# MLP down passes: seven products in place of eight for the first two input blocks and each pair of output groups

## The chip, the cores and the metric

The kernel runs on one core of a Trainium2 chip. Five engines of the core work side by side: TensorE (PE in the profile, with PEld for the loading of its stationary operand), VectorE (DVE), ScalarE (ACT), GpSimd (POOL) and SyncE (SP), which here only issues DMAs. Matmuls write to PSUM, eight banks of 128 x 512 float32; all else lies in SBUF. The metric is the device time of one execution in microseconds (us).

## The reference, cut to what matters

Two decoder layers on 256 tokens of width 2048 in float32. Each has a mixer and then a gated MLP with a short causal convolution:

```python
def conv_ffn(h, w_up, conv_w, conv_b, w_down):      # h: (1, 256, 2048)
    z = h @ w_up                                    # 2048 x 11264
    zp = jnp.pad(z, ((0, 0), (2, 0), (0, 0)))
    z = sum(conv_w[j] * zp[:, j:j + 256] for j in range(3)) + conv_b
    a, b = jnp.split(z, 2, axis=-1)
    return (jax.nn.silu(a) * b) @ w_down            # 5632 x 2048

for l in range(2):
    x = x + mixer(l, rms_norm(x, mix_norm[l]))
    x = x + conv_ffn(rms_norm(x, ffn_norm[l]), ...)
```

The change is in the last product, `(...) @ w_down`.

## The kernel before, in words

Float32 accuracy is built from three fast products. Each operand is split in a rounded high part and the rest (h and l), and a product is ah*bh + ah*bl + al*bh, three matmuls. Activations are split once and kept; weights are split as they come: ScalarE makes `wh` (line 185) and VectorE makes `wl = w - wh` (line 186). `halves` does both, `weights` (196) loads a tile of 512 KB on SP's queue and calls it.

`three` (162) hands out the buffers w, wh and wl of one weight tile and counts a turn. In the MLP (`deep["more"] == 2`), from turn 13 on, turns that are 1 or 3 modulo 5 take them from the pool fw (2 buffers of each kind), the others from wp (5 buffers of w, 3 of wh and of wl).

`project_four` (356) computes 256 tokens x 512 output columns: two PSUM banks, one for each half T of the tokens, and steps of two input blocks of 128. A step loads one weight tile (2 input blocks x 512 columns) and issues 2 (T) x 2 (input blocks) x 3 = 12 matmuls of 128x512, in lines 369 to 371. The stationary operand is the activation block, the moving one the weights.

`ffn` (1298) is the MLP of a layer. `up(j0)` computes four hidden blocks with two calls of project_four (8 steps each) and lets convolution, gate and split run beside later work, as generators that `tick` moves on by one piece each step; the result is appended to `hid`, a list of split hidden blocks of 128 features. `down(k0, hid, ...)` (1406) takes n of them, and for each of the four groups q of 512 output columns runs project_four over the n blocks (n/2 steps) and adds the two banks to `y` in SBUF (the first pass copies them, line 1424, later ones add, line 1426). STEPS sets the order: 4 ups, a down pass of 12 blocks; 3 ups, 12 blocks; 4 ups, 12 blocks; and the last 8 blocks. In the last pass `add_y` transposes each finished group of y and adds it to the residual x; in the last pass of the second MLP, group 3 is computed another way, block by block with `project` (301), and its sum of the earlier passes is added by `add_y(3, False)` ahead of the pass.

The order on each engine is the compiler's, from the dependences that it finds. Besides them `in_order` chains all w loads, all wh and all wl in written order, and `held` keeps an operation behind the last wl written so far.

Of the kernel before, what the change touches and what calls it, by code (L numbers as in the profile page):

```python
# [55 lines left out]
def tile_trunk(ctx: ExitStack, tc: tile.TileContext, x, pp_d, cst_d, mlev_d, msk_d,  # L56
# [105 lines left out]
    def three(n):  # L162
# [7 lines left out]
        w = wpool.tile([P, n], F32, tag="w", name=nm("w"), bufs=nw)  # L170
# [184 lines left out]
    def project_four(w4, acts, n, k0=0, ks=None, ps=None, more=False):  # L355

        begun = ps is not None
        ps = ps or [pm.tile([P, 512], F32, tag="pm", name=nm("pm")) for _ in range(2)]
        ks = ks or range(0, n, 2)
        for k in ks:  # L360
            tick()
            lo = (k0 + k) * P
            wh, wl = weights(w4[:, :, lo:lo + 2 * P].rearrange("m p c -> p m c"), 1024, 4)
            for T in range(2):
                for i in range(2):
                    a = acts(k + i) if callable(acts) else acts[k + i]
                    ah, al = a[:, T * P:(T + 1) * P], a[:, S + T * P:S + (T + 1) * P]
                    h, l = (by_rows(t, i) for t in (wh, wl))
                    PE.matmul(to_rows(ps[T]), ah, h, start=not begun and k + i == ks[0], stop=False)  # L369
                    PE.matmul(to_rows(ps[T]), ah, l, start=False, stop=False)  # L370
                    deep["mm"] = deep["last"] = PE.matmul(to_rows(ps[T]), al, h, start=False,  # L371
                                                          stop=not more and k + i == ks[-1] + 1)
        return ps

# [72 lines left out]
    class Norm:  # L447
        def __init__(self, col, turn=False):
# [4 lines left out]
            self.acc = cp.tile([P, S], F32, tag="acc", name=nm("acc"), bufs=2)  # L453
# [844 lines left out]
    def ffn(l, norm, last):  # L1298
        es = ExitStack()
        hp = es.enter_context(tc.tile_pool(name="fp", bufs=1))  # L1300
        deep.update(pool=es.enter_context(tc.tile_pool(name="fw", bufs=1)), turn=0, more=2)
        A = norm.a
# [7 lines left out]
        def four(j0):  # L1310
            ps = project_four(w_up[l, j0:j0 + 4], A, KT)
# [26 lines left out]
        def up(j0):  # L1338
# [12 lines left out]
            zb, eb = four(HT + j0)  # L1351
# [54 lines left out]
        def down(k0, hid, first, final):  # L1406
            n = len(hid)
            for q in range(4):
                if last and final and q == 3:
                    parts = None  # L1410
                    for m in range(4 * q, KT):
                        end = m == KT - 1
                        ps = project(w_dn[l, m], hid, chunks=(n,), k0=k0, parts=parts)
# [6 lines left out]
                ps = project_four(w_dn[l, 4 * q:4 * q + 4], hid, n, k0)  # L1420
# [6 lines left out]
                if final:  # L1427
                    add_y(q, True)

        j0, k0, hid = 0, 0, []  # L1430
        for g, (now, ahead) in enumerate(STEPS):
            while 4 * j0 < k0 + 4 * (now + ahead):
                up(4 * j0)
                j0 += 1
            n, final = 4 * now, g == len(STEPS) - 1
            if last and final:
                add_y(3, False)
            while len(hid) < k0 + n:
                tick()
            down(k0, hid[k0:k0 + n], g == 0, final)  # L1440
            k0 += n
        if last:
# [89 lines left out]
```

## Time and profile before

| | |
|---|---|
| median of 3 runs | 2166.17 us (2165.52 to 2166.69) |
| profiled execution, span | 2164.7 us |
| TensorE busy | 2160.1 us, 10736 matmuls |
| VectorE busy | 1610.1 us |
| ScalarE busy | 1307.4 us |
| GpSimd busy | 473.8 us |
| HBM read | 435.24 MB, 202 GB/s over the span |
| matmuls on `hid` (down passes), each of lines 369 to 371 | 688 |

The profile is of one execution. A group's row gives line, engine, operation, output and inputs, shapes and count, then the busy time in us and the mean in ns of one, then the idle time of the engine ahead of them and what ended it. A row of the timeline gives start and duration in us, engine, line and operation, and in brackets the idle time just before with its releaser. A row of the windows gives the window, then the busy time and count for PE, PEld, DVE, ACT and POOL, the granted clock, the DMA share and GB/s.

### The profile page before, as it was taken

The page shows a single profiled execution, that of the slowest core. Times are in us where ns is not written, and L with a number is a line of the kernel's source. Part 1 is how long each engine was busy: PE and PEld are TensorE (multiplying, and loading weights), DVE is VectorE, ACT ScalarE, POOL GpSimd, SP SyncE. Part 2 cuts the span into 40 slices and gives each one's busy share as a digit, 9 for nine tenths or more (in the row PEclk, how much of TensorE's full clock was granted, in tenths as well). Part 3 has the DMA queues.
Part 4 walks back from the last instruction along what each step waited for, and adds up shares of the span by engine and source line. Part 5 has one row for each costly group of instructions (what it writes and reads, how often), then busy time and mean ns, then how long its engine had stood idle before and what let it go on. Part 6 is the DMA issues. An engine that isn't in the chain of part 4 may idle for free.

```text
span 2164.7 us, 32175 instructions
## 1 busy us (share of the span) xinstructions
PE 2160.1 (100%) x10736; PEld 1895.8 (88%) x10736; DVE 1610.1 (74%) x2313; ACT 1307.4 (60%) x1888; POOL 473.8 (22%) x865
## 2 busy tenths in 40 slices
PE   9999999999999999999999999999999999999999
PEld 8888888888888888888888888888888888888888
DVE  7888768877577657776987787877786577667766
ACT  6677766666456545654565556766666466456652
POOL 0362231212012002111233443221211012012103
PEclk9999999999999999999999999999999999999999
DMA  8755777778667767776777767787777677766766
GB/s 300 224 171 174 223 222 237 237 227 241 216 214 223 225 209 216 225 239 207 249 232 222 246 201 214 221 243 220 242 234 224 201 236 217 227 214 211 243 213 194
DMA packets 492327, 483.60 MB, mean 223 GB/s; under 512 B 115360, under 2 KB 460080, under 8 KB 492032
## 3 DMA queue, kind: packets, MB, share of 16 engines
q1 hardware_dynamic: 465888, 453.41, 66.8%
q0 software_dynamic: 24832, 25.98, 5.2%
q10 hardware_dynamic: 1440, 2.15, 0.3%
q8 instruction: 84, 1.38, 0.3%
q14 instruction: 83, 0.68, 0.1%
HBM read 435.24 MB, written 2.11 MB: 202 GB/s over the span
## 4 chain that ended last, share of the span: by engine, by line
PE 100%; DMA 0%; ACT 0%; DVE 0%; SPq 0%; issue 0%; ACTq 0%
PE pm L369 27%; PE pm L370 27%; PE pm L371 27%; PE pm L350 5%; PE pm L352 4%; PE pm L351 4%; PE pm L236 1%; PE pm L315 1%; PE pm L318 1%; PE pm L260 1%; PE pm L325 0%; PE px L1110 0%; PE px L1163 0%; PE lv L829 0%; PE px L1107 0%; PE px L617 0%
## 5 line engine op out<-in xcount | busy, mean ns | idle before, releaser
L186 DVE TENSOR_TENSOR wl<-w,wh 128x1024 fp32r<-128x1024 f32 (+1 forms) x820 | 992.5, 1218 | 456.8 <-ACT wh L185 441.3
L185 ACT ACTIVATE wh<-w 128x1024 fp32r<-128x1024 f32 (+1 forms) x820 | 857.4, 1050 | 622.3 <-PE pm L371 449.3
L369 PE MATMUL pm<-wh,a 128*128 128x512 f32 x1728 | 655.7, 379 | 0.0
L370 PE MATMUL pm<-wl,a 128*128 128x512 f32 x1728 | 655.1, 379 | 0.0
L371 PE MATMUL pm<-wh,a 128*128 128x512 f32 x1728 | 654.9, 379 | 0.0
L391 POOL DMA_DIRECT2D zt<-tmp x413 | 223.6, 549 | 1135.2 <-DVE tmp L382 1047.6
L370 PEld LDWEIGHTS pm<-wl,a 128*128 128x128 f32 x1728 | 326.6, 189 | 46.7 <-DVE wl L186 0.7
L369 PEld LDWEIGHTS pm<-wh,a 128*128 128x128 f32 x1728 | 326.6, 189 | 46.3
L371 PEld LDWEIGHTS pm<-wh,a 128*128 128x128 f32 x1728 | 326.6, 189 | 46.3
L369 PE MATMUL pm<-wh,hid 128*128 128x512 f32 x688 | 260.8, 379 | 0.0
L370 PE MATMUL pm<-wl,hid 128*128 128x512 f32 x688 | 260.8, 379 | 0.0
L371 PE MATMUL pm<-wh,hid 128*128 128x512 f32 x688 | 260.8, 379 | 0.0
L350 PE MATMUL pm<-wh,a 128*128 128x512 f32 x416 | 158.5, 381 | 0.0
L351 PE MATMUL pm<-wl,a 128*128 128x512 f32 x416 | 157.7, 379 | 0.0
L352 PE MATMUL pm<-wh,a 128*128 128x512 f32 x416 | 157.7, 379 | 0.0
L370 PEld LDWEIGHTS pm<-wl,hid 128*128 128x128 f32 x688 | 130.0, 189 | 18.5
L369 PEld LDWEIGHTS pm<-wh,hid 128*128 128x128 f32 x688 | 130.0, 189 | 18.4
L371 PEld LDWEIGHTS pm<-wh,hid 128*128 128x128 f32 x688 | 130.0, 189 | 18.4
L1333 ACT ACTIVATE conv<-zt,pp 128x256 f32<-128x256 f32 x176 | 95.8, 589 | 64.1 <-DMA zt<-tmp 48.5
L391 POOL DMA_DIRECT2D turn<-tmp x159 | 86.4, 551 | 206.0 <-DVE tmp L382 173.0
L1334 DVE SCALAR_TENSOR_TENSOR conv<-zt,pp,conv 128x255 f32<-128x255 f32 x176 | 80.1, 480 | 47.8 <-ACT conv L1333 47.5
L382 DVE STREAM_TRANSPOSE tmp<-z 128x512 f32<-128x512 f32 x120 | 98.6, 855 | 6.1 <-ACT z L1319 4.2
(259 smaller groups left out, 2207.2 us busy)
## 6 DMA issues: line engine op xcount, KB each, us to landing
w<-in_w_up SPq DMA_DIRECT2D x352, 512.0 KB, 5.1
w<-in_w_dn SPq DMA_DIRECT2D x176, 512.0 KB, 4.9
w<-in_w_cqkv SPq DMA_DIRECT2D x96, 512.0 KB, 5.0
w<-in_w_abo SPq DMA_DIRECT2D x32, 512.0 KB, 4.9
w<-in_w_cg SPq DMA_DIRECT2D x32, 512.0 KB, 5.0
w<-in_w_co SPq DMA_DIRECT2D x32, 512.0 KB, 4.9
zt<-tmp SPq DMA_DIRECT2D x416, 32.0 KB, 2.5
zt<-tmp POOLq DMA_DIRECT2D x413, 32.0 KB, 2.5
```

The lines of the kernel that those rows point to most:

```text
L185: r = deep["wh"] = SC.activation(wh, w, AF.Copy)
L186: deep["wl"] = V.tensor_tensor(wl, w, wh.bitcast(F32), ALU.subtract)
L350: PE.matmul(to_two(ps[T]), ah, h, start=k + i == 0, stop=False)
L351: PE.matmul(to_two(ps[T]), ah, l, start=False, stop=False)
L352: deep["last"] = PE.matmul(to_two(ps[T]), al, h, start=False, stop=k + i == KT - 1)
L369: PE.matmul(to_rows(ps[T]), ah, h, start=not begun and k + i == ks[0], stop=False)
L370: PE.matmul(to_rows(ps[T]), ah, l, start=False, stop=False)
L371: deep["mm"] = deep["last"] = PE.matmul(to_rows(ps[T]), al, h, start=False, stop=not more and k + i == ks[-1] + 1)
L382: r = V.transpose(tmp.rearrange("p (b m i t) -> p b m i t", b=4, m=4, t=2)[:, :, :, :, T], src(T).rearrange("p (m b j) -> p b m j", m=4, b=4))
L391: queues[(a + b) % len(queues)].dma_start(dst[BLK * b:BLK * (b + 1), :, a * n:(a + 1) * n], tmp[BLK * a:BLK * (a + 1), b * 4 * n:(b + 1) * ...
L1333: held(SC.activation(c, z, AF.Identity, bias=pp[:, cb:cb + 1], scale=w(2)))
L1334: V.scalar_tensor_tensor(c[:, 1:], z[:, :S - 1], w(1), c[:, 1:], ALU.mult, ALU.add)
```

## The change

For a pair of token halves, a pair of input blocks and a pair of output groups, the product is one of 2x2 blocks: A (activations a11, a12, a21, a22; the first index is the token half) times B (weights). Eight block products become seven by a scheme of Strassen's kind: some products are of sums of blocks, and the four results are sums of products. `seven` does this for input blocks k0 and k0+1 of each pass and groups 0 and 1, then 2 and 3. The other input blocks go on in project_four, which adds to the same four banks. A bank is begun by a product (x0, x3), or by copying another bank (x1, from x0 by ScalarE) or a sum of a bank and a copy in SBUF (x2 and x3, by VectorE), and later products add to it.

The run of seven is a generator cut in four stages, and project_four moves it on before each of its last three steps and finishes it after them (`inset`): for groups 0 and 1 within the last call of the last up ahead of the pass (for the last pass, within group 3 of the pass before), for groups 2 and 3 within group 1 of the same pass. In the last pass of the second MLP groups 2 and 3 are left as before. `combos` makes the sums of activation blocks, once a pass, in the place of the x blocks 12 to 15, which are put aside in DRAM on POOL's queue and fetched back on SP's (`x_back`) in the last pass. In the ups too project_four now draws its banks from both PSUM pools (`two_banks`).

The diff, cut to its core (calls in up and four that only hand `inset` on are left out, and flags `skip_group_check` too):

```diff
-    def three(n):
+    def three(n, raw=True):
...
-        w = wpool.tile([P, n], F32, tag="w", name=nm("w"), bufs=nw)
+        w = wpool.tile([P, n], F32, tag="w", name=nm("w"), bufs=nw) if raw else None
...
+    def two_banks():
+        ring[0] += 2
+        pick = (lambda: pm.tile([P, 512], F32, tag="pm", name=nm("pm"))) if ring[0] % 8 < 4 else bank
+        return [pick() for _ in range(2)]
+    AHEAD = 4
+    def project_four(w4, acts, n, k0=0, ks=None, ps=None, more=False, inset=None):
...
         for k in ks:
+            if inset is not None and k > ks[-1] - 2 * AHEAD + 2:
+                next(inset, None)
...
+        for _ in inset or ():
+            pass
         return ps
+
+    def combos(dst, a, tmp, pause):
+        r, c = tmp[:, 0:512], tmp[:, 512:1024]
+        for i in range(2):
+            held(V.tensor_tensor(r[:, i * S:(i + 1) * S], a[i][:, 0:S].bitcast(F32),
+                                 a[i][:, S:2 * S].bitcast(F32), ALU.add), "wl")
+        a11, a21, a12, a22 = (r[:, i * P:(i + 1) * P] for i in range(4))
+        s3, s1, s2, s4 = (c[:, i * P:(i + 1) * P] for i in range(4))
+        yield
+        held(V.tensor_tensor(s3, a11, a21, ALU.subtract), "wl")
+        V.tensor_tensor(s1, a21, a22, ALU.add)
+        V.tensor_tensor(s2, a22, s3, ALU.subtract)
+        V.tensor_tensor(s4, a12, s2, ALU.subtract)
+        yield
+        held(SC.activation(dst[:, 0:512], c, AF.Copy))
+        yield
+        held(V.tensor_tensor(dst[:, 512:1024], c, dst[:, 0:512].bitcast(F32), ALU.subtract), "wl")
+
+    def seven(w4s, a, comb, lo, ps, spare):
+        (x1, x0), (x2, x3) = ps
...
+        tick()
+        first, second, third = (three(1024) for _ in range(3))
+        for (w, _, _), src in zip((first, second), sl):
+            in_order("w", nc.sync.dma_start(w.rearrange("p (m c) -> p m c", m=4), src))
+        b1, b2, t = first[0], second[0], third[0]
+        parts(*first)
+        then(V.tensor_tensor(block(t, 0), block(b2, 1), block(b2, 0), ALU.subtract))
+        then(V.tensor_tensor(block(b2, 0), block(b2, 0), block(b1, 0), ALU.subtract))
+        then(V.tensor_tensor(block(t, 1), block(t, 0), block(b1, 0), ALU.add))
+        parts(*second)
+        product(x0, a11h, a11l, first[1:], 0, True)
+        SC.activation(x1, x0, AF.Copy)
+        product(x3, *sums(1), second[1:], 0, True)
+        SC.activation(spare, x3, AF.Copy)
+        yield
+        parts(*third)
+        product(x1, a12h, a12l, first[1:], 1)
+        product(x0, *sums(2), third[1:], 1)
+        V.tensor_tensor(x2, x0, spare, ALU.add)
+        yield
+        tick()
+        _, wh, wl = three(1024, False)
+        then(V.tensor_tensor(block(t, 1), block(b1, 1), block(t, 1), ALU.subtract))
+        parts(t, wh, wl, 1)
+        product(x0, *sums(0), third[1:], 0)
+        V.tensor_tensor(x3, x0, spare, ALU.add)
+        yield
+        product(x2, *sums(3), second[1:], 1)
+        product(x0, a22h, a22l, (wh, wl), 1)
...
-            self.acc = cp.tile([P, S], F32, tag="acc", name=nm("acc"), bufs=2)
+            self.acc = cp.tile([P, S], F32, tag="acc", name=nm("acc"), bufs=1)
...
+        def x_back():
+            t = cp.tile([P, 4, S], F32, tag="x12", name=nm("x12"))
+            nc.sync.dma_start(t, xs)
...
+        def begin(q, k0):
+            ps = two_banks(), two_banks()
+            def run():
+                while comb[0] != k0:
+                    tick()
+                spare = hp.tile([P, 512], F32, tag="z", name=nm("p5"), bufs=2)
+                yield from seven([w_dn[l, 4 * (q + i):4 * (q + i) + 4] for i in range(2)], hid[k0:k0 + 2],
+                                 comb[1], k0 * P, ps, spare)
+            return ps, run()
...
-                ps = project_four(w_dn[l, 4 * q:4 * q + 4], hid, n, k0)
+                inset, ks, ps = None, range(2, n, 2), None
+                if q == 1 and not (last and final):
+                    later, inset = begin(2, k0)
+                elif q == 3 and after:
+                    coming, inset = begin(0, k0 + n)
+                if last and final and q == 2:
+                    ks = None
+                else:
+                    ps = begun[q % 2]
+                ps = project_four(w_dn[l, 4 * q:4 * q + 4], acts, n, k0, ks=ks, ps=ps, inset=inset)
```

`product` issues the three matmuls of one block product; `parts` splits a weight tile, or one block of it, with `halves`; `then` puts a sum of weight blocks in the chain of wl; `sums(i)` is a combination from combos.

More of the change, by code (lines that the diff above doesn't have):

```diff
@@ L1301, in ffn @@
         deep.update(pool=es.enter_context(tc.tile_pool(name="fw", bufs=1)), turn=0, more=2)
+        dp = es.enter_context(tc.tile_pool(name="xs", bufs=1, space=bass.MemoryType.DRAM))
+        deep["seven"] = True
         A = norm.a
@@ L1350, in up @@
             start(gate())
-            zb, eb = four(HT + j0)
+            zb, eb = four(HT + j0, inset)
             def fill():
```

86 lines of the change are left out of this document (71 added, 15 removed).

## Prediction

> **What bounds the kernel now.** I read the page first, then the waits of TensorE, then the order of time around the places that change.
>
> ```profile
> span 2164.7 us, 32175 instructions
> PE 2160.1 (100%) x10736; PEld 1895.8 (88%) x10736; DVE 1610.1 (74%) x2313; ACT 1307.4 (60%) x1888; POOL 473.8 (22%) x865
> PEclk9999999999999999999999999999999999999999
> PE 100%; DMA 0%; ACT 0%; DVE 0%; SPq 0%; issue 0%; ACTq 0%
> ```
>
> TensorE (PE) is busy in every slice, at full granted clock, and the chain that ended last is PE from end to end. "Busy" is no proof by itself, since a pipelined matmul's end is modelled, so I also asked who PE waited for:
>
> ```profile
> PE warm L143 <- DVE ones L85: 1.1, 1, 1.1
> ```
>
> That is the whole answer: one wait of 1.1 us at the start. So a matmul taken away shortens the kernel by what it spaces, unless a new wait appears; and any new wait on PE lengthens it one for one. What one matmul spaces is not the duration in its group:
>
> ```profile
> L369 PE MATMUL pm<-wh,hid 128*128 128x512 f32 x688 | 260.8, 379 | 0.0
> ```
>
> ```profile
> 521.36 0.38 PE L369 MATMUL pm<-wh,a 128*128 128x512 f32 x1
> ...
> 523.95 0.38 PE L369 MATMUL pm<-wh,hid 128*128 128x512 f32 x1
> ```
>
> Between these two starts lie the 12 matmuls of one step of project_four (2 token halves x 2 input blocks x 3 partial products): 2.59 us, so 0.2158 us each. The 379 ns of the group overlaps the next matmul by 0.16 us and would overstate every saving by three quarters.
>
> **The saving.** Per pair of output groups, the two input blocks cost 2 x 12 = 24 matmuls now; seven products of three matmuls are 21. An inset (one run of seven) serves two groups, so a full down pass has two: 4 passes x 2 in the first MLP, 8. In the second MLP's last pass groups 2 and 3 stay as they are, so 7. That is 15 insets x 3 = 45 matmuls, 45 x 0.2158 = 9.7 us. The profiled execution has span 2164.7 against a median of 2166.17 us, so 1.5 us lie outside the span or between executions; I take the change off the median: 2156.5 us if nothing else gets on the path. The Trainium skill, page "TensorE: Matmul & The Clock Gate", section "Back-to-back issue gap", says that a stream of weight loads and 512-column matmuls sustains about 131 ns per matmul; by it the saving would be only 5.9 us (an estimate from that page). The trace does not agree: 216 ns, in just such a stream.
>
> **What is added, and where it lies.** Rows for the prices:
>
> ```profile
> L186 DVE TENSOR_TENSOR wl<-w,wh 128x1024 fp32r<-128x1024 f32 x812 | 987.1, 1223 | 453.1 <-ACT wh L185 437.8 <-DMA zt<-tmp 9.5 <-DMA turn<-tmp 1.4
> L185 ACT ACTIVATE wh<-w 128x1024 fp32r<-128x1024 f32 x812 | 852.6, 1054 | 619.5 <-PE pm L371 449.3 <-PE pm L352 72.2 <-ACT wh L185 25.4
> ...
> L382 DVE STREAM_TRANSPOSE tmp<-z 128x512 f32<-128x512 f32 x120 | 98.6, 855 | 6.1 <-ACT z L1319 4.2 <-ACT z L512 1.6
> ...
> L1426 DVE TENSOR_TENSOR y<-y,pm 128x512 f32<-128x512 f32 x46 | 29.9, 682 | 1.8 <-PE pm L371 1.8
> ...
> L470 DVE TENSOR_TENSOR acc<-acc,sq 128x256 f32<-128x256 f32 x60 | 25.0, 417 | 1.1
> ...
> L840 DVE COPY_PREDICATED st<-msk,lv 128x128 f32<-128x128 uint16 x40 | 12.9, 321 | 0.5
> ...
> L1190 DVE TENSOR_TENSOR z<-z,ss 128x512 f32<-128x512 f32 x16 | 10.3, 686 | 0.1
> ...
> L1424 ACT ACTIVATE y<-pm 128x512 f32<-128x512 f32 x16 | 9.5, 596 | 5.5 <-PE pm L371 5.5
> ```
>
> VectorE, per inset: the weights are split 3.5 times instead of twice (+1.5 x 1.223 = 1.83), four sums of weight blocks (4 x 0.686 = 2.74), two sums into a bank (2 x 0.682 = 1.36): 5.9 us. Per pass, the combined activations (combos): 2 x 0.417 + 4 x 0.321 + 0.686 = 2.8 us, eight times. Together 15 x 5.9 + 8 x 2.8 = 111 us against 2164.7 - 1610.1 = 555 us idle. ScalarE, per inset: 1.5 x 1.054 + two copies of a bank at 0.596 = 2.8 us, and 0.6 per combos: 47 us against 857 idle. As totals both fit. No row shows a copy from bank to bank; between zero on the path (hidden) and 0.6 us each I take hidden: both copies (1.2 us) stand beside an ordinary step of 2.59 us. The same step length covers each bank sum (0.68 us), which PE must await before it writes x0 again. If that cover went, the price would be 15 x 2 x 0.68 = 20 us, which is why the order of the work decides.
>
> DMA: the two weight loads per inset are the two that the ordinary steps issued, so SP's queue issues as many as before. The only new transfers are the four x blocks put aside and fetched back.
>
> ```profile
> w<-in_w_dn SPq DMA_DIRECT2D x176, 512.0 KB, 4.9
> ...
> cb<-cd POOLq DMA_DIRECT2D x4, 512.0 KB, 5.7
> ```
>
> One goes out on POOL's queue early in each MLP, with two ups or more (16 steps each) before the first inset reads what takes its room, and one comes back on SP's: 512 KB, some 5 us each. Behind the fetch on SP stand weight loads; it waits for the last product that reads comb. Weight tiles are issued several steps ahead, so I cost both at nothing; without that cover it is 2 x 4.9 us. In the last pass add_y(3) now stands behind the fetch, with ten steps (26 us) of groups 0 to 2 still to go. The raw tiles of F and T (below) stay until the fourth block sum, two of the seven places for w; five are left for loads that land in two steps: nothing. The single buffer for acc costs nothing either: the old sum is read at the start of an MLP, the new one begun in its last pass.
>
> **The wait that can replace the saving.** The groups say that VectorE idles for ScalarE's wh (437.8 of 453.1 us) and ScalarE for PE (449.3 of 619.5): the splits run as far ahead as buffers allow.
>
> ```profile
> 549.63 0.38 PE L371 MATMUL pm<-wh,hid 128*128 128x512 f32 x1
> ...
> 549.85 0.38 PE L369 MATMUL pm<-wh,hid 128*128 128x512 f32 x1
> ...
> 550.09 1.06 ACT L185 ACTIVATE wh<-w 128x1024 fp32r<-128x1024 f32 x1 [1.58 <-PE pm L371]
> ...
> 551.18 1.23 DVE L186 TENSOR_TENSOR wl<-w,wh 128x1024 fp32r<-128x1024 f32 x1 [1.42 <-ACT wh L185]
> ```
>
> A step ends and the next begins at 549.85; 0.24 us later the freed buffer is being filled, and 2.56 us after 549.85 (551.18 + 1.23 - 549.85) its wl is ready. In the MLP there are five places for wh and wl: three in wp, two in fw for turns that are 1 or 3 modulo 5 (line 166). So a buffer is ready 4 x 2.59 - 2.56 = 7.8 us before it is used. An inset holds places much longer: its second weight tile S serves the second and the sixth product, with three ordinary steps between. Call the tiles in order F, S, T, r, r', Q, r'' (r: ordinary steps, Q: the split without a load). PE's written order is F S r F T r' T r'' S Q.
>
> In which pool each falls depends on F's turn. With 16 turns per up, 5 per group and 4 per inset I count F = 62, 76, 138, 152, 230, 244, 258, 268 in the first MLP, the same without 268 in the second. If F is 2 modulo 5 (62, 152), S and r' hold both places of fw, and r'' needs one; if 3 (138, 258, 268), S, T and r' hold all of wp, and r'' needs one. In these nine insets r'' can't be split before r' has ended. Count from that end: wh 0.24 to 1.30; VectorE first adds x3 (fifth product ends at 3 x 0.2158 + 0.16 = 0.81, plus 0.68 = 1.49), then wl to 2.71. In written order r'' needs wl with its second matmul, at 0.65 + 0.22 = 0.86: a wait of 1.85 us. If instead the compiler lets the sixth and seventh products go ahead (both are independent of r''; the seventh from 1.49, when x3 is read), they end at 2.14 and wl is due at 2.36 but there at 2.71; against the undisturbed 1.94 + 0.22 = 2.16 the wait is 0.55 us.
>
> Is PE's order the written one? On ScalarE the order is not:
>
> ```profile
> 552.68 1.06 ACT L185 ACTIVATE wh<-w 128x1024 fp32r<-128x1024 f32 x1 [1.53 <-PE pm L371]
> ...
> 553.93 0.60 ACT L1424 ACTIVATE y<-pm 128x512 f32<-128x512 f32 x1 [0.19 <-PE pm L371]
> ...
> 555.23 0.60 ACT L1424 ACTIVATE y<-pm 128x512 f32<-128x512 f32 x1 [0.70 <-PE pm L371]
> ```
>
> The eviction at 555.23 is written ahead of all splits of the next group, yet that group's matmuls follow without a gap, so its splits were put before it: the compiler orders by readiness. I take the same for PE. The loss is then 9 x 0.55 = 5.0 us, and the forecast 2166.2 - 9.7 + 5.0 = 2161.5 us. Its own range: 0.25 to 0.85 us per wait, 2159.0 to 2164.1.
>
> In the other six insets r'' finds a place earlier. From F's first matmul: the third product ends at 4.53; Q's half split runs on ScalarE 4.77 to 5.37, r'' wh to 6.42, wl to 7.64, due at 8.63: 1.0 us in hand, no loss.
>
> **Rivals.**
> - **Written order on PE** (slower). S, Q and r'' stay as written: nine waits of 1.85 us are 16.7, so 2166.2 - 9.7 + 16.7 = 2173.2 us. It decides against the change from a wait of 9.7 / 9 = 1.08 us on. For it: in the before trace PE has nothing that it could have put forward, so its order is untested. Against: ScalarE's order above. The Trainium skill (same page, Part 2) says that matmuls start and complete in program order and only weight loads are pulled ahead; by it nothing in the chip would heal a late r''. PE hardly waits in this trace, which therefore shows nothing on it.
> - **VectorE too full around the insets** (no change). Rows of two such places, with DVE the third engine:
>
> ```profile
> 510.00:524.00 14.00, 14.00 (x67) 12.26 (x66) 10.33 (x15) 9.28 (x14) 1.09 (x3) 1.00 0.88 260
> ...
> 975.00:990.00 15.00, 15.00 (x72) 13.12 (x71) 8.45 (x8) 6.17 (x6) 0.00 (x0) 1.00 0.66 214
> ```
>
> At the end of an up VectorE has 3.7 us free of 14 while an inset adds 5.9; the lead must give the rest. At 975 it has 6.5 free, so not every inset is tight. If two transpositions (2 x 0.855 = 1.71) stand in front of the last wl everywhere, the six lose 1.71 - 1.0 = 0.7 each and the nine their 0.55: 4.2 + 5.0 = 9.2, so 2165.7 us.
> - **All hidden** (faster). If places are freed sooner than I read, or S's product goes earlier still, nothing is lost: 2156.5 us.
> - That the work isn't saved at all I hold out of question: 21 matmuls stand in the code where 24 stood.
>
> **How the numbers follow.** A measurement of this kernel tells about 0.2%, 4.3 us, from no change: faster is below 2161.8, slower above 2170.5. Forecast 0.42 (its range crosses 2161.8 slightly above its middle: 0.28 faster, 0.14 same), all hidden 0.14, VectorE full 0.19, written order 0.25. Faster 0.28 + 0.14 = 0.42, same 0.14 + 0.19 = 0.33, slower 0.25. The range takes in all hidden, and written order with a little above it: 2156 to 2174, leaving out under 0.2.
>
> **What would show it.** 10691 matmuls instead of 10736. Waits of PE for wl or wh at r'' at the ends of the ups and in the second group, of about 0.5 us in nine insets (right), 1.85 us (written order), in all fifteen (VectorE), or none. Waits on the copies or bank sums would mean that the cover failed, and a wait for w that the loads did; either makes the forecast wrong. Matmuls that space other than 0.216 us would make the saving wrong.

## The result and the profile after

The changed kernel takes 2197.34 us (median of 4 runs, 2194.91 to 2198.46) against 2166.43 us (4 runs, 2165.52 to 2167.17) for the kernel before beside it: 1.014 of it, 95% interval 1.0126 to 1.0155. It is 30.9 us slower, and the forecast of 2161.5 us was wrong, outside its range. From the page of the profile after, the span, the engines and the chain that ended last:

```profile
span 2196.2 us, 32373 instructions
PE 2169.6 (99%) x10691; PEld 1885.5 (86%) x10691; DVE 1704.7 (78%) x2489; ACT 1343.8 (61%) x1956; POOL 476.4 (22%) x867
PE 78%; DVE 10%; DMA 4%; ACT 3%; SPq 2%; issue 2%; POOL 1%; ACTq 0%; DVEq 0%; POOLq 0%
```

The 45 matmuls are gone. But the chain that was TensorE from end to end now runs through VectorE, DMA and ScalarE for a good fifth of its length. PE's list of waits, one single entry before, shows where (in all, times, longest, in us; its first eight rows):

```profile
PE pm L325 <- ACT wh L185: 5.1, 1, 5.1
PE pm L383 <- DVE wl L186: 3.4, 7, 0.8
PE pm L350 <- ACT wh L185: 2.5, 2, 2.1
PE pm L381 <- ACT wh L185: 1.7, 2, 1.1
PE px L383 <- DVE wl L186: 1.6, 4, 1.0
PE pm L434 <- DVE wl L186: 1.6, 2, 0.8
PE px L434 <- DVE wl L186: 1.5, 2, 0.8
PE px L433 <- ACT wh L185: 1.3, 1, 1.3
```

Every one of these is a wait for a split of weights (wh or wl). The whole list comes to some 20 us. The lost time counted below is larger, because the list counts a wait only from the modelled end of the matmul ahead (0.16 us after the next one could have started) and because a matmul at a lower clock waits for nothing. In the kernel after, lines 381 to 384 are the matmuls of ordinary steps and 433 to 435 those of the seven products; none waits for a copy of a bank or a bank sum, nor directly for a load. Where the time went by stage is read from the first matmul of the same stretch in both timelines of PE. After (start, duration), from the first up of MLP 1 to the start of mixer 2, of MLP 2 and of the last group:

```profile
358.59 0.38 PE L381 MATMUL pm<-wh,a 128*128 128x512 f32 x1
...
1053.21 0.38 PE L350 MATMUL pm<-wh,a 128*128 128x512 f32 x1
...
1492.92 0.38 PE L381 MATMUL px<-wh,a 128*128 128x512 f32 x1
...
2178.02 1.23 PE L325 MATMUL pm<-hid,wh 128*128 128x256 f32 x4 [5.14 <-ACT wh L185]
```

and before:

```profile
357.99 0.38 PE L369 MATMUL pm<-wh,a 128*128 128x512 f32 x1
...
1041.97 0.38 PE L350 MATMUL pm<-wh,a 128*128 128x512 f32 x1
...
1476.98 0.38 PE L369 MATMUL pm<-wh,a 128*128 128x512 f32 x1
...
2150.38 0.61 PE L325 MATMUL pm<-hid,wh 128*128 128x256 f32 x4
```

MLP 1 takes 694.6 us for 684.0 (+10.6), mixer 2 up to MLP 2 takes 439.7 for 435.0 (+4.7, though nothing in it was changed), MLP 2 up to its last group 685.1 for 673.4 (+11.7), and the rest, by the spans, 18.2 for 14.3 (+3.9).

For the places I take each gap between the starts of 512-column matmuls, subtract the undisturbed 0.2158 us, and add up what is left from 340 us on: "lost time" below. Before it is 0.6 us in all. After it is 37.2 us, nearly all in two kinds of place: some 24 us around the insets (2.9 us at 549 to 563, 2.0 at 738, 3.0 at 937, 4.6 at 970, 1.9 at 1653, 2.7 at 1686, 2.0 at 1874, 2.4 at 2103, and smaller ones), 11.3 us in and after the last passes of the two MLPs (1.3 at 1048, 4.7 at 1058 to 1075, 5.3 at 2178), and 2 us elsewhere. Behind 2178 the 256-column matmuls of the last group, which this sum leaves out, take 3.2 us longer from the first start to the last (13.76 us for 10.61), so the last passes come to 14.5 us. 30.9 us slower and 9.7 us of matmuls saved make 40.6 us to find; 37.2 + 3.2 = 40.4 us are found.

**One inset closely.** PE's timeline at the inset in group 1 of the first pass, where the first tile F is used at 547.77 and the second, S, from 548.75:

```profile
547.77 0.38 PE L433 MATMUL px<-wh,hid 128*128 128x512 f32 x1
...
548.75 0.48 PE L433 MATMUL pm<-wh,comb 128*128 128x512 f32 x1 [0.17 <-ACT wh L185]
550.01 0.48 PE L434 MATMUL pm<-wl,comb 128*128 128x512 f32 x1 [0.78 <-DVE wl L186]
```

VectorE's timeline ahead of it (lines 447 to 449 are block sums of weights, 497, 1432 and 1455 the MLP's own work):

```profile
543.59 1.22 DVE L186 TENSOR_TENSOR wl<-w,wh 128x1024 fp32r<-128x1024 f32 x1
544.72 0.86 DVE L497 TENSOR_TENSOR hid<-conv,hid 128x256 fp32r<-128x256 f32 x2
545.51 0.45 DVE L1432 SCALAR_TENSOR_TENSOR conv<-zt,pp,conv 128x255 f32<-128x255 f32 x1
545.89 0.68 DVE L447 TENSOR_TENSOR w<-w 128x512 f32<-128x512 f32 x1
...
546.88 0.68 DVE L448 TENSOR_TENSOR w<-w,w 128x512 f32<-128x512 f32 x1
...
547.81 0.68 DVE L449 TENSOR_TENSOR w<-w,w 128x512 f32<-128x512 f32 x1
548.73 1.23 DVE L186 TENSOR_TENSOR wl<-w,wh 128x1024 fp32r<-128x1024 f32 x1 [0.24 <-ACT wh L185]
```

F's wl is ready at 544.81, only 3.0 us before the first product, and S's wl ends at 549.96, when PE has been waiting 0.78 us. Between the two splits VectorE is never idle for more than a quarter of a microsecond. The windows of the two kernels (PE, PEld, VectorE, ScalarE and GpSimd busy with counts, clock, DMA share, GB/s) show the same. After:

```profile
540.00:556.00 16.00, 14.94 (x65) 11.68 (x64) 14.58 (x26) 10.56 (x17) 0.00 (x0) 1.00 0.48 157
```

Before, in the stretch with the same operations of the gate:

```profile
535.00:551.00 16.00, 16.00 (x76) 14.02 (x75) 13.23 (x22) 11.33 (x16) 0.00 (x0) 1.00 0.74 239
```

VectorE had 2.8 us free of 16 here even before the inset's 5.9 us came.

But VectorE did not set F's lead of 3.0 us alone. SP's queue ahead of this inset (line 487 moves transposed blocks, line 444 loads F and S):

```profile
532.45 5.48 SPq L487 DMA_DIRECT2D zt<-tmp  x8
538.03 1.08 SPq L444 DMA_DIRECT2D w<-in_w_dn  x2
```

F's load stands behind eight moves and lands 3.8 us after its issue, at 541.87. With 1.06 us for wh and 1.22 for wl, the split can't be ready before 544.2; it was at 544.81. Four of the fifteen insets have loads like these, issued right behind seven or eight moves and landed 5.9 to 7.2 us before the first product (at 547.8, 968.0, 1684.2 and 2101.4; 10.0 us or more at the other eleven). These four lose 2.9, 4.6, 2.8 and 2.4 us, 12.7 of the 24. In the 6 us or so between a load and its product must fit F's split, two or three block sums and S's split, in this order. Late loads, the order and the volume of VectorE's work can all act here, and none of the experiments below moves these loads alone.

The queue then stands still behind these loads, from 541 to 557 (its row of waits, in all, times, longest):

```profile
SPq L198 <- DVE w L463: 15.8, 1, 15.8
```

Until the fourth block sum (line 463) has read F and T, these two hold two raw places for w. The next load is issued 15.8 us later, and ScalarE then waits 2.40 us for it at 560.73. The same happens at the inset of 1686; what it cost TensorE is not isolated.

**The last passes.** SP's queue of the kernel after, just ahead of the last group (start, time to issue, what is moved):

```profile
2165.57 5.11 SPq L487 DMA_DIRECT2D zt<-tmp  x8
2170.79 0.53 SPq L1498 DMA_DIRECT2D out<-x  x1
2171.36 0.92 SPq L198 DMA_DIRECT2D w<-in_w_dn  x2
```

and ScalarE's timeline:

```profile
2176.91 1.06 ACT L185 ACTIVATE wh<-w 128x1024 fp32r<-128x1024 f32 x1 [8.92 <-DMA w<-in_w_dn]
```

Eight moves of a transposed group stand ahead of weight loads on the in-order queue, the loads land late, and the last group's first matmul waits 5.14 us. The same moves took 5.12 us before (below), with longer groups to hide behind. From this came the first theories: late queues in the last passes, and at the insets either the volume of VectorE's work, its order (S's wh at 547.64 starts as L448, which overwrites a block of S, ends at 547.56), or the places held by S, T and F.

SP's queue before, for comparison:

```profile
2132.30 5.12 SPq L391 DMA_DIRECT2D zt<-tmp  x8
2137.52 1.49 SPq L198 DMA_DIRECT2D w<-in_w_dn  x3
```

### The profile page after: what moved, and what is told of

Its sections match the earlier page's. It is cut to its first block, busy times and chain, and to the rows that moved or that the text cites. A ratio compares the mean times of both kernels' runs of the same rounds, so it can differ in the third digit from the quotient of the medians.

```text
span 2196.2 us, 32373 instructions
## 1 busy us (share of the span) xinstructions
PE 2169.6 (99%) x10691; PEld 1885.5 (86%) x10691; DVE 1704.7 (78%) x2489; ACT 1343.8 (61%) x1956; POOL 476.4 (22%) x867
## 4 chain that ended last, share of the span: by engine, by line
PE 78%; DVE 10%; DMA 4%; ACT 3%; SPq 2%; issue 2%; POOL 1%; ACTq 0%; DVEq 0%; POOLq 0%
PE pm L383 13%; PE pm L384 13%; PE pm L381 13%; PE px L383 7%; PE px L384 7%; PE px L381 7%; PE pm L350 4%; PE pm L352 4%; PE pm L351 4%; DVE wl L186 4%; SPq L487 2%; DMA zt<-tmp 2%; PE pm L236 1%; ACT wh L185 1%; PE pm L315 1%
## 5 line engine op out<-in xcount | busy, mean ns | idle before, releaser
L186 DVE TENSOR_TENSOR wl<-w,wh 128x1024 fp32r<-128x1024 f32 (+1 forms) x850 | 1014.1, 1206 | 345.1 <-ACT wh L185 334.7
L383 PE MATMUL pm<-wl,a 128*128 128x512 f32 x1024 | 389.0, 380 | 2.7 <-DVE wl L186 2.7
L381 PE MATMUL pm<-wh,a 128*128 128x512 f32 x1024 | 388.8, 380 | 1.2 <-ACT wh L185 1.1
L384 PE MATMUL pm<-wh,a 128*128 128x512 f32 x1024 | 388.1, 379 | 0.0
L383 PE MATMUL px<-wl,a 128*128 128x512 f32 x704 | 267.1, 379 | 0.0
L384 PE MATMUL px<-wh,a 128*128 128x512 f32 x704 | 266.8, 379 | 0.0
L381 PE MATMUL px<-wh,a 128*128 128x512 f32 x704 | 266.7, 379 | 0.0
L383 PEld LDWEIGHTS pm<-wl,a 128*128 128x128 f32 x1024 | 193.5, 189 | 32.9 <-DVE wl L186 5.8
L381 PEld LDWEIGHTS pm<-wh,a 128*128 128x128 f32 x1024 | 193.5, 189 | 29.6 <-ACT wh L185 2.3
L384 PEld LDWEIGHTS pm<-wh,a 128*128 128x128 f32 x1024 | 193.5, 189 | 27.2
L350 PE MATMUL pm<-wh,a 128*128 128x512 f32 x416 | 158.6, 382 | 2.6 <-ACT wh L185 2.5
L351 PE MATMUL pm<-wl,a 128*128 128x512 f32 x416 | 157.6, 379 | 0.6 <-DVE wl L186 0.6
L352 PE MATMUL pm<-wh,a 128*128 128x512 f32 x416 | 157.4, 379 | 0.0
L383 PEld LDWEIGHTS px<-wl,a 128*128 128x128 f32 x704 | 133.0, 189 | 19.7 <-DVE wl L186 0.9
L381 PEld LDWEIGHTS px<-wh,a 128*128 128x128 f32 x704 | 132.9, 189 | 19.3 <-ACT wh L185 0.5
L384 PEld LDWEIGHTS px<-wh,a 128*128 128x128 f32 x704 | 133.1, 189 | 18.9
L383 PE MATMUL px<-wl,hid 128*128 128x512 f32 x292 | 112.2, 384 | 1.6 <-DVE wl L186 1.6
```

Source lines behind the costliest of these rows:

```text
L186: deep["wl"] = V.tensor_tensor(wl, w, wh.bitcast(F32), ALU.subtract)
L350: PE.matmul(to_two(ps[T]), ah, h, start=k + i == 0, stop=False)
L351: PE.matmul(to_two(ps[T]), ah, l, start=False, stop=False)
L352: deep["last"] = PE.matmul(to_two(ps[T]), al, h, start=False, stop=k + i == KT - 1)
L383: PE.matmul(to_rows(ps[T]), ah, l, start=False, stop=False, skip_group_check=loose)
```

## The experiments

Times are medians; each ratio stands against the kernel before in the same job, about 2166.3 us. In the diffs `USE(g, pair)` says whether pass g of an MLP does its first (0) or second (1) pair of groups by seven products; where it says no, the steps are as before.

**Insets of the last passes left out** (`no_last`).

```diff
+def USE(g, pair):
+    return g < 3
```

> The last pass of each MLP is as before; 12 insets stay, in the first three passes. Queue theory (in the last passes the groups are three steps instead of four, each still puts eight moves on SyncE's queue, and weight loads stand behind them): the waits after the last passes go (in the changed kernel 1.3 us within the last pass and 4.7 us at the start of the second mixer, 5.3 and 3.2 us in the last output group), 14.5 us, against 3 x 0.65 us of saving given up: about 2185 us. Places theory of the prediction, or a loss spread evenly over the insets (40.6 / 15 = 2.7 us each, net 2.06): three insets fewer, about 2191 us.

Measured 2183.19 us, ratio 1.0078 (1.0063 to 1.0093): 14.2 us less than the whole change, though it saves 9 matmuls fewer. The lost time is 26.4 us, none of it in or after the last passes. So the three insets of the last passes, with the shorter groups and the fetch of x that come with them, cost far more each than the other twelve. The queue theory's figure was about 2185 us, but this run does not tell queue, groups and fetch apart. The rest is lost at the insets of passes 0 to 2.

**One pair alone** (`ups_only`, `downs_only`).

```diff
+def USE(g, pair):
+    return pair == 0      # ups_only: groups 0 and 1
+    return pair == 1      # downs_only: groups 2 and 3
```

> Only groups 0 and 1 of each pass use seven products (8 insets, at the end of an up or of the pass before). Lead theory (where VectorE and ScalarE are still busy with the gates of the last up, in group 1, the splits of an inset come too late; at the end of an up there is room): these eight insets lost 5.5 us together in the changed kernel's trace, saving 5.2; with some 10 us of the last-pass waits left, about 2176 us. Even loss per inset: 2166.4 + 8 x 2.06 = 2183 us. Places theory: inset turns 2 or 3 modulo 5 lose wherever they stand, so neither kind is better.

> Only groups 2 and 3 of each pass use seven products (7 insets, run within group 1). Lead theory: these insets lost 17 us in the changed kernel's trace, saving 4.5; the end of the first MLP another 6; the tail of the kernel is as before: about 2185 us, most of the loss of the whole change. Even loss per inset: 2166.4 + 7 x 2.06 = 2181 us, and ups_only above it.

Measured 2183.49 us, 1.0078 (1.0063 to 1.0093), and 2176.78 us, 1.0048 (1.0031 to 1.0065). The lead theory's figures, 2176 and 2185 us, both missed; `ups_only` came out at the 2183 us of an even loss per inset. Groups 0 and 1 alone lose 10.4 us at their eight insets, where they lost 6.5 in the whole change, and 7.3 us more at 2153 to 2164, just ahead of the last group. Groups 2 and 3 alone lose 8.2 us at their seven insets, where they lost 17.4, and 5.7 us in and after the last pass of the first MLP. So only one kind of inset loses less when it stands alone. It loses nothing in the first pass of either MLP, where the whole change lost 2.9 us (549); there F's load now stands ahead of the eight moves and lands 16.2 us before its use. The two groups ahead of it are a step longer too, and no run tells these two differences apart.

**The block sums' order** (`sums_first`, `sums_last`, `free_s`). In the first, sums 1 and 2 stand ahead of F's split and sum 3 behind S's; in the second, S's split comes ahead of all sums; in the third, only the write to S is taken away, so that S's wh need not follow a sum (its wl still does, by the chain of wl).

```diff
 sums_first
-        parts(*first)
         then(... L447 ...); then(... L448 ...)
-        then(... L449 ...)
+        parts(*first)
         parts(*second)
+        then(... L449 ...)
 sums_last and free_s
-        then(V.tensor_tensor(block(b2, 0), block(b2, 0), block(b1, 0), ALU.subtract))
+        then(V.tensor_tensor(block(t, 1), block(b2, 0), block(b1, 0), ALU.subtract))
 sums_last alone
         parts(*first)
+        parts(*second)
         then(... L447 ...)
...
-        parts(*second)
```

> The first two sums of weight blocks are put ahead of the first split, the third behind the second split; work and buffers are the same. Lead theory (the second tile's split waits for first split, sum, sum in one chain): ScalarE no longer idles between the two splits, 1.4 us off each chain, the waits at the second product shrink: 5 to 10 us off, about 2190 us. Places theory or plain volume of VectorE work: no change, 2197 us.

> free_s with its three sums behind the second split in the chain, so that the second product waits for two splits and nothing else; VectorE's work per inset as in the changed kernel (the output is not the reference's). Chain theory: as no_sums, 2183 us. Volume theory: as free_s, 2191 us or so.

> The sums of weight blocks are all made, but the second sum is written to a block of the third tile and not back to the second, whose unsummed blocks are split (the output is not the reference's). VectorE's work is that of the changed kernel; only the dependence of the second tile's split on two sums is gone. Chain theory: as no_sums, within 5 us of it (about 2183 us). Volume theory: no change, 2197 us.

Measured 2193.99 us, 1.0127 (1.0112 to 1.0142); 2196.47 us, 1.0138 (1.0121 to 1.0155); 2191.20 us, 1.012 (1.0105 to 1.0135). Lost: 37.2, 36.7 and 36.0 us. The four runs of `sums_first` spread from 2190.2 to 2198.2 us, so its 3.4 us are not clear of the whole change's own spread (2194.9 to 2198.5); three of the four runs of `free_s` lie below it. With S's split wholly free of the sums (`sums_last`) nothing is won, but that does not clear the order: the wait moves on to T, whose split must follow the sums. At the same inset, ScalarE's splits and PE's fourth product of the inset (line 191 is wh, 456 the third sum, 439 begins a product, here that of T) are now

```profile
549.88 2.00 ACT L191 ACTIVATE wh<-w 128x1024 fp32r<-128x1024 f32 x2 [0.35 <-DVE w L456]
550.99 0.48 PE L439 MATMUL px<-wh,comb 128*128 128x512 f32 x1 [1.02 <-ACT wh L191]
```

So these three orders win 6 us at most, and each still has the sums ahead of a split that is soon needed. They don't show what a kernel without that chain would win.

**The four block sums left out** (`no_sums`).

```diff
-        then(V.tensor_tensor(block(t, 0), block(b2, 1), block(b2, 0), ALU.subtract))
-        then(V.tensor_tensor(block(b2, 0), block(b2, 0), block(b1, 0), ALU.subtract))
-        then(V.tensor_tensor(block(t, 1), block(t, 0), block(b1, 0), ALU.add))
...
-        then(V.tensor_tensor(block(t, 1), block(b1, 1), block(t, 1), ALU.subtract))
```

> The four sums of weight blocks per inset are left out (the third and fourth split take unsummed blocks, so the output is not the reference's); same splits, products, buffers. Chain theory (the second tile's split stands behind first split, sum, sum, and all later splits behind it): with the chain cut, the second split follows the first at once, inset waits fall by more than half: about 2180 us. It takes 41 us of VectorE's work away too, so volume theory says the same.

Measured 2182.57 us, 1.0076 (1.0061 to 1.0091), 14.8 us less than the whole change; lost 22.7 us, of it 9.6 at the insets of passes 0 to 2, where the whole change loses 22.7. Leaving out 15 x 4 x 0.68 = 41 us of VectorE's work more than halves the loss at the insets. It also leaves out the chain in which splits wait for sums, so it doesn't tell volume from order, as its expectation said. At the four insets with late loads F's load still lands 6.1 to 7.1 us before the first product, yet only 2.7 us are lost there for 12.7: what a late load costs hangs on the sums, by their order or their volume.

**VectorE's work alone, put into the kernel before** (`before_load`). Nine sums of 0.68 us (6.1 us) go with the splits of the last three steps at the 15 places; no product is changed and no buffer held longer.

```diff
+    def loaded(w, wh, wl):
+        for _ in range(3):
+            in_order("wl", V.tensor_tensor(wl[:, 0:512], w[:, 0:512], w[:, 512:1024], ALU.add))
+        return halves(w, wh, wl)
...
-            wh, wl = weights(..., 1024, 4)
+            wh, wl = weights(..., 1024, 4, loaded if load and k > ks[-1] - 6 else halves)
```

> The kernel before, with nothing but VectorE work added at the fifteen places of the insets: three sums of 128x512 in each of the three steps, ahead of the split, 9 x 0.69 = 6.2 us per place (an inset adds 5.9). They write into the place of wl, which the split then overwrites. No seven products, no buffers held, nothing more on ScalarE. Volume theory (VectorE has no room there for another 6 us): the waits of the insets appear, some 15 to 25 us, 2181 to 2191 us. Chain or buffer theories (it is the order of an inset's splits, or the places that it holds): the lead of the splits covers it, under 2170 us.

Measured 2176.70 us, 1.0044 (1.0029 to 1.0059), 10.4 us slower, between the two expectations; lost 10.0 us, in the same kind of wait as in the change, 6.3 us of it at the fifteen places and 3.0 at the start of mixer 2. Its first row of PE's waits:

```profile
PE pm L376 <- DVE wl L186: 4.1, 7, 1.0
```

So VectorE's added work by itself makes PE wait for wl. It is the one cause shown in isolation, and at the places of the insets it is worth 6.3 of the 24 us.

**A place less, and both together** (`before_4`, `before_4load`). In the kernel before, wh and wl get four places in place of five (in `three`); the second has the added VectorE work too.

```diff
-            if deep["more"] == 2 and deep["turn"] > 12 and deep["turn"] % 5 in (1, 3):
-                wpool, pool, nw, ns = deep["pool"], deep["pool"], 2, 2
+            if deep["more"] == 2 and deep["turn"] > 12:
+                if deep["turn"] % 4 == 1:
+                    pool, ns = deep["pool"], 1
+                if deep["turn"] % 5 in (1, 3):
+                    wpool, nw = deep["pool"], 2
```

> Control: the kernel before with four places for wh and for wl in the MLPs instead of five (loads unchanged). The splits then run at most 3 x 2.59 - 2.56 = 5.2 us ahead instead of 7.8. Nothing in this kernel needs more for long: 2166 to 2170 us.

> before_load (VectorE work of an inset at its fifteen places, 2176.7 us) with four places for wh and wl instead of five. If the rest of the insets' loss comes from the places that an inset holds for three steps, which cuts the lead out of which VectorE's extra work is paid: the 10 us of before_load grow towards the insets' 26 us or beyond, 2185 to 2195 us. If places do not matter: before_load plus what before_4 loses, 2177 to 2181 us.

Measured 2173.63 us, 1.0033 (1.0021 to 1.0045), and 2185.52 us, 1.0088 (1.0074 to 1.0101). The loss of 7.3 us by a place less was not expected, but none of the lost time that the trace shows of it (4.6 us) is at the places of the insets. Most of it, 2.6 us, is at the start of mixer 2, with no group shortened; so TensorE can come to wait there without a short group. With the added work, PE's first row of waits is

```profile
PE pm L379 <- DVE wl L189: 7.6, 14, 1.1
```

fourteen waits for seven. At the places of the insets 10.6 us are lost for 6.3 in `before_load`, in one profiled execution each: the same VectorE work costs more there where one place is missing. In total the two effects only little more than add up (17.7 against 19.2 us), a difference inside the intervals.

**The moves on another queue** (`moves_pool`). The residual's moves go to POOL's queue twice and SP's once.

```diff
-                       NINE if q == 3 else (nc.sync, nc.gpsimd))
+                       NINE if q == 3 else (nc.gpsimd, nc.sync, nc.gpsimd))
```

> The changed kernel; in the last passes 11 of a group's 16 transposing moves go on POOL's queue and 5 on SyncE's, instead of 8 and 8 (groups 0 and 1, in the first MLP also 2). Queue theory: weight loads come 3 x 0.64 = 1.9 us earlier behind each burst, so the waits after the last passes (14.5 us) shrink by about half where these groups decide: 2190 us. Otherwise no change or slower by later moves: 2197 us or more.

Measured 2190.26 us, 1.0109 (1.0094 to 1.0124), 7.1 us less, as the queue theory had it; lost 29.1 us. The insets lose nearly what they lose in the change (23.3 us for 23.8), the last passes 7.8 us for 14.5, with the slower last group counted in both. The last group's wait, 5.1 us in the change, is now

```profile
PE pm L331 <- ACT wh L191: 1.6, 1, 1.6
```

**Shorter groups alone** (`before_short`). The kernel before leaves out the first step of the last-pass groups that the change shortens, 6 x 12 matmuls or 15.5 us of work; nothing is put in its place.

```diff
+                ks = range(2, n, 2) if final and (q < 2 or not last) else None
-                ps = project_four(w_dn[l, 4 * q:4 * q + 4], hid, n, k0)
+                ps = project_four(w_dn[l, 4 * q:4 * q + 4], hid, n, k0, ks=ks)
```

> The kernel before with the first two input blocks left out of the last passes (groups 0 to 3 in the first MLP, 0 and 1 in the second), so that these groups have three steps as in the changed kernel, and no product in their place (the output is not the reference's). Work left out: 6 steps x 2.59 = 15.5 us, so 2150.8 us if nothing waits. Queue theory (short groups with as many moves): most of the 14.5 us of waits after the last passes appears here too, 2160 to 2165 us. If the insets cause them: 2151 to 2154 us.

Measured 2156.84 us, 0.9956 (0.9941 to 0.9971). Without new waits it would be 2150.8, so groups of three steps cost 6.0 us for themselves, between the two expectations and less than the 14.5 us lost there in the change. There the inset's work falls on the same stretch, and the fetch of x waits 3.4 us on SP's queue, in the second MLP, for a product of the inset; no run isolates either.

**The generators' pieces later** (`late_gates`, `no_last_late`). My rival to all this was that the convolution's wait for its transposed input, larger after, blocks ScalarE's in-order queue ahead of the splits. Three more empty pieces in `empty` move the convolution later; the second kernel leaves out the last passes' insets as well.

```diff
-                for _ in range(LAG):
+                for _ in range(LAG + 3):
```

> The changed kernel with the gates of an up three steps later (LAG + 3 in empty). Queue-head theory: on ScalarE a gate's first conv operation stands ahead of the split that the next matmuls need and waits there for its transposing moves (in ups_only 2.1 us at the inset where 4.2 us were lost); three steps later the moves have landed. The waits at the insets (about 26 us in the changed kernel) fall by half or more, those after the last passes (14.5 us) stay: 2180 to 2186 us. Volume theory (VectorE has too much to do): 2195 us or more, since the work is the same.

> no_last (12 insets, last passes as before) with the gates three steps later too. If both causes are right and add up: the 14.5 us of the last passes are gone already at 2183 us, half or more of the inset waits go as well: 2165 to 2172 us. Volume theory: 2182 us.

Measured 2202.58 us, 1.0174 (1.0157 to 1.0191), and 2189.15 us, 1.0108 (1.0093 to 1.0123): 5 to 6 us slower each. The convolution's group in the change (after the last bar: idle time ahead, and what ended it) was

```profile
L1431 ACT ACTIVATE conv<-zt,pp 128x256 f32<-128x256 f32 x176 | 97.3, 592 | 92.8 <-DMA zt<-tmp 73.7 <-DMA w<-in_w_up 19.1
```

and with the later pieces

```profile
L1437 ACT ACTIVATE conv<-zt,pp 128x256 f32<-128x256 f32 x176 | 103.4, 589 | 67.6 <-DMA zt<-tmp 46.7 <-DMA w<-in_w_up 20.5 <-issue 0.2
```

The wait fell by 27 us and the time rose. That wait was not on the path; the theory falls.

**The gate's product on GpSimd** (`gates_tt`), to take 88 products off VectorE.

```diff
-                    V.tensor_tensor(b, b, ca[i], ALU.mult)
+                    nc.gpsimd.tensor_tensor(b, b, ca[i], ALU.mult)
```

> The changed kernel with the product of the two gate halves (88 times 128x256, 0.42 us each on VectorE) on GpSimd. Volume theory from the other side: VectorE has 34 us less to do, 1.7 us in the stretch before many insets; their waits shrink by 3 to 8 us, 2189 to 2194 us. A cost of GpSimd's slower product or of its queue, which also issues the moves, speaks against it: 2197 us or more.

Measured 2238.89 us, 1.0338 (1.0322 to 1.0354). The product's group shows why this says nothing on volume:

```profile
L1461 POOL TENSOR_TENSOR conv<-conv,conv 128x256 f32<-128x256 f32 x88 | 109.5, 1251 | 226.1 <-DVE conv L1439 180.5 <-ACT wh L191 45.2 <-ACT y L1577 0.5
```

1.25 us for one where VectorE took 0.42, in an in-order queue with the moves, which now stand behind a product that waits (226 us idle ahead of them in all).

**Only the insets that cost least** (`few`): groups 2 and 3 of the first two passes of each MLP.

```diff
+def USE(g, pair):
+    return pair == 1 and g < 2
```

> Seven products only where downs_only lost least: groups 2 and 3 of the first two passes of each MLP, 4 insets. In downs_only these lost 0, 1.0, 0 and 0.7 us against 4 x 0.65 = 2.6 us saved: 2165.4 us, hardly to be told from before. Volume theory: an inset gains only where VectorE has room, so not slower than before. If an inset costs by itself, whatever runs beside it (2.06 us each in the changed kernel): 2174.6 us.

Measured 2166.64 us, 1.0002 (0.9993 to 1.001): 3.5 us lost (0.6 before) against 12 x 0.2158 = 2.6 us saved. No version here that computes the whole product beats the kernel before. More places for wh and wl in the changed kernel, and loads of the insets ahead of the moves, were not tried.

## Why the prediction was wrong, point by point

- **The saving**: right. 10691 matmuls, and undisturbed ones still space 0.2158 us. (By its own sum the forecast's range starts at 2158.7 us, not 2159.0; nothing hangs on it.)
- **TensorE's order**: right, and with it the rival of the written order falls. A later product is put ahead of the rest of a step: line 433 at 526.72 stands among the L381 matmuls of the timeline below.
- **Copies and bank sums hidden**: right; PE waits for none. The margin is thin: in `sums_last` it waits 1.7 us for two of the copies.
- **"So a buffer is ready 4 x 2.59 - 2.56 = 7.8 us before it is used"**: this step failed. It was read at 549.85, where VectorE was idle 1.4 us ahead of the split, and taken for all fifteen places. It is the most that five places allow. Over the steps of MLP 1 in the kernel before, the time from the end of a split to the first matmul that uses its tile has a median of 7.5 us, but is 6.3 us at 550 and 2.5 us at 962, where the inset stands that later lost most (970). At the inset of 547.77 the lead in hand was 3.0 us, since its loads came late, and an inset asks 5.9 us of VectorE.
- **"As totals both fit"**: the same error from the other side, 111 us of new work against 555 us idle. Where it was added VectorE had 2.8 us free in 16. `before_load` shows that volume alone costs 6.3 us at these places; `no_sums` takes away volume and order together, and the three orders leave the question open. The window I quoted as a roomy place, 975 to 990 with 6.5 us free, holds no inset: in that pass the steps that take one in group 1 run from 961.6 to 969.3. Just there VectorE is full in the kernel before:

```profile
956.00:960.00 4.00, 4.00 (x21) 3.49 (x20) 4.00 (x9) 1.73 (x4) 0.00 (x0) 1.00 0.98 336
960.00:964.00 4.00, 4.00 (x20) 3.52 (x19) 4.00 (x5) 2.51 (x3) 0.00 (x0) 1.00 0.07 12
```

At that inset in the kernel after, VectorE is busy 3.34 and 3.97 us of two windows of 4 (968 to 976, last section), and 4.6 us are lost.
- **The nine insets with F at 2 or 3 modulo 5**: wrong. I predicted that r'' would wait 0.55 us there. At F = 62, PE's timeline is

```profile
526.18 0.70 PE L381 MATMUL px<-wh,a 128*128 128x512 f32 x2
526.72 0.38 PE L433 MATMUL px<-wh,hid 128*128 128x512 f32 x1
...
527.37 0.38 PE L381 MATMUL px<-wh,hid 128*128 128x512 f32 x1
527.60 0.48 PE L383 MATMUL px<-wl,a 128*128 128x512 f32 x1
```

with all but 0.2 us of it undisturbed, while F = 230 and 244 in the first MLP, two of the six that should lose nothing, lose most (3.0 and 4.6 us). The nine lose 7.8 us together where 5.0 were forecast, the six 16.1 where none was. The waits stand at S's wh and wl and in the ordinary steps around the products, wherever the lead ran out.
- **DMA "at nothing"**: wrong. The count of issues was right, their place was not. In the last passes, with one step fewer in each group, loads stand behind 5.1 us of moves; `moves_pool` (7.1 us less) shows it. At four other insets the inset's own loads stand behind such moves and leave 5.9 to 7.2 us; they lose half of the 24 us. And the raw places of F and T, also put at nothing, hold the load queue for 15.8 us at two insets, at a cost that no run isolates.
- **The rival "VectorE too full around the insets"** named a part of the mechanism. Its price of 9.2 us was built on the same 7.8 us lead, less two transpositions; the fifteen insets cost about 24.

Shown: the loss is at the insets (24 us) and in the last passes (14.5 us). VectorE's work alone makes 6.3 us of the first; without the four block sums less than half of it is left. Of the second, short groups by themselves make 6.0 us, and moves on another queue take back 6.7; the two may overlap. Open: how the other 18 us at the insets divide among the loads behind moves, the splits that wait for sums, the places that F, S and T hold for three steps, and ScalarE's own 2.8 us an inset; no run isolates them.

## What to carry to other kernels

Where a fast engine feeds the bound one through a few buffers, judge added work by the free time within the few microseconds that the buffers bridge, at each place where it is put, and not by the idle total nor by a lead read in a quiet stretch. Test one insertion alone and all together: here one kind lost less alone, the other more. For each insertion, and for each group of steps that gets shorter, look at the in-order DMA queue again for what stands ahead of the next loads. An experiment that only moves a chain of work to the next consumer, as `sums_last` did, does not show that the chain is harmless.

## What the runs showed of the hardware that was not expected

TensorE's clock fell to half after quite short waits. Windows of the kernel after (the clock is the third figure from the end), at the inset of 970 and at the last group:

```profile
968.00:972.00 4.00, 1.91 (x8) 1.11 (x8) 3.34 (x6) 2.95 (x4) 0.00 (x0) 1.00 0.00 1
972.00:976.00 4.00, 4.00 (x12) 3.22 (x11) 3.97 (x5) 2.84 (x5) 0.00 (x0) 0.57 0.00 0
976.00:980.00 4.00, 4.00 (x20) 3.50 (x19) 1.97 (x5) 0.87 (x2) 0.00 (x0) 1.00 0.64 203
2178.00:2184.00 6.00, 5.95 (x26) 5.65 (x27) 4.88 (x8) 2.75 (x3) 2.67 (x5) 0.50 0.33 89
```

PE's rows with a wait in the first of them:

```profile
970.16 0.48 PE L433 MATMUL px<-wh,comb 128*128 128x512 f32 x1 [1.31 <-ACT wh L185]
971.42 0.48 PE L434 MATMUL px<-wl,comb 128*128 128x512 f32 x1 [0.78 <-DVE wl L186]
```

After two waits of 1.31 and 0.78 us the matmuls space 0.43 us from 972.50 to 975.48, about 2 us of the 4.6 lost at that inset. After the 5.14 us wait the clock is half for the whole window of 6 us, which makes 3.2 of the 3.9 us that the end of the kernel is longer. So a wait of PE is not always paid one for one, as I had assumed.

The Trainium skill, page "TensorE: Matmul & The Clock Gate", section "What's actually happening", gives half clock after at least one idle window of about 3.4 us, and full clock after a busy one. The return after 3.3 us at 975 agrees; the fall at 972 does not, since no wait there is longer than 1.31 us and PE was busy for 1.91 of the 4 us before.

GpSimd took 1.25 us for a product of 128x256 for which VectorE took 0.42 us.
